# Prefix logsumexp over time: three time steps per partition, exponentials written over the input, chunks interleaved, one DMA queue

## The chip, the cores and the metric

The kernel runs on one core of one Trainium2 chip. The metric is the device time of one execution in microseconds, as the median of several runs. A profile of one execution is shown as well; its span is counted from its first to its last recorded instruction.

## The reference

```python
B, S, D = (4, 4096, 4128)                      # x is float32, normally distributed
out[:, 0, :] = x[:, 0, :].copy()
for t in range(1, S):
    mx = np.maximum(out[:, t - 1, :], x[:, t, :])
    out[:, t, :] = mx + np.log(np.exp(out[:, t - 1, :] - mx) + np.exp(x[:, t, :] - mx))
```

For every batch and column the output at time t is the logarithm of the sum of exp(x) over all times up to t. The kernel computes it as Ln(prefix sum of Exp(x)). Input and output are 270.53 MB each, so at least 541 MB cross between HBM and SBUF.

## The kernel before

**Tiles.** One tile holds 256 consecutive time steps of one batch, all 4128 columns: partition p holds the two rows 2p and 2p+1 (`R = 2`), which are one contiguous run of 33 KB in HBM. There are 4 batches of 16 tiles, 64 in all. A tile is loaded in float32 into `xt` (pool `xpool`, 5 buffers), its exponentials are written in float16 to `et` (pool `epool`, 2 buffers), and the result is written in float32 back into `xt`, from where it is stored.

**Prefix sum on TensorE.** The columns are cut in four chunks of 1024 (`CH`) and a tail of 32; a matmul covers 512 columns (`MM`), so that every matmul of a chunk comes as a pair. For a chunk, `head` adds into one PSUM tile `pt` (pool `pmain`, 3 buffers[...]): a triangular matrix `incl` times the exponentials of row 0, a strictly triangular `excl` times those of row 1, and, except in the first tile of a batch, `last` times the carry. The carry is a float16 copy of the running sum; `last` picks its partition 127. ScalarE then takes Ln of `pt` into row 0 of `xt` (line 98). `second` adds the exponentials of row 1 with an identity (`ident`), takes Ln into row 1 (line 105), and VectorE copies `pt` to the carry (line 106). The 32-column tail does the same in a small PSUM tile `qt` (lines 124 and 125). All matmuls are recorded under the helper `mm`, line 80.

**Order of the work.** `tc.manual_schedule()` keeps each engine's instructions in the order in which the program emits them. The main loop emits for each tile: its load on SP's DMA queue (line 135), one Exp over the whole tile of 2 x 4128 columns on ScalarE (line 139), and then the scan of the tile before. Within a scan, `head` of chunk c is emitted ahead of `second` of chunk c-1. The store is issued on the queue of GpSimd (POOL) at the end of the scan (line 126). A load waits until the store that used its buffer five tiles before has landed.

Of the kernel before, what the change touches and what calls it, by code (L numbers as in the profile page):

```python
# [1 line left out]

# [4 lines left out]

FP32 = mybir.dt.float32
FP16 = mybir.dt.float16
ACT = mybir.ActivationFunctionType  # L10
P = 128
R = 2
CH = 1024
MM = 512


def _constants(nc, pool):


    def tri(base, name):  # L20
        t = pool.tile([P, P], FP16, name=name)
        nc.gpsimd.memset(t, 1.0)

        nc.gpsimd.affine_select(  # L24
            out=t, in_=t, pattern=[[1, P]], compare_op=mybir.AluOpType.is_ge,
            fill=0.0, base=base, channel_multiplier=-1,
        )
        return t

    def ones_where_zero(base, mult, step, name):  # L30
        t = pool.tile([P, P], FP16, name=name)
        nc.gpsimd.memset(t, 0.0)
        nc.gpsimd.affine_select(  # L33
            out=t, in_=t, pattern=[[step, P]], compare_op=mybir.AluOpType.not_equal,
            fill=1.0, base=base, channel_multiplier=mult,
        )
        return t

    return (
        tri(0, "incl"),  # L40
        tri(-1, "excl"),
        ones_where_zero(0, 1, -1, "ident"),
        ones_where_zero(-(P - 1), 1, 0, "last"),
    )


@with_exitstack
def kernel(
    ctx: ExitStack,
    tc: tile.TileContext,  # L50
    x: bass.AP,
    out: bass.AP,
):

    nc = tc.nc
    B, S, D = x.shape
    rows = P * R
    n_t = S // rows  # L60
    assert S % rows == 0
    n_main = D // CH
    tail = D - n_main * CH
    t0 = n_main * CH

    nc.scalar.preload_act_table_set("natural_log_exp_and_others")  # L66
    consts = ctx.enter_context(tc.tile_pool(name="consts", bufs=1))
    incl, excl, ident, last = _constants(nc, consts)

    xpool = ctx.enter_context(tc.tile_pool(name="xpool", bufs=5))  # L70
    epool = ctx.enter_context(tc.tile_pool(name="epool", bufs=2))
    cpool = ctx.enter_context(tc.tile_pool(name="cpool", bufs=1))
    pmain = ctx.enter_context(tc.tile_pool(name="pmain", bufs=3, space=bass.MemoryType.PSUM))
    ptail = ctx.enter_context(tc.tile_pool(name="ptail", bufs=2, space=bass.MemoryType.PSUM))

    carry = [cpool.tile([P, CH], FP16, name=f"carry{c}") for c in range(n_main)]
    carry_t = cpool.tile([P, tail], FP16, name="carry_t") if tail else None

    def mm(pt, w, rhs, start, stop):
        nc.tensor.matmul(pt, lhsT=w, rhs=rhs, start=start, stop=stop, skip_group_check=True)  # L80

    def scan(b, k, xt, et):
        first = k == 0

        def head(c):
            pt = pmain.tile([P, CH], FP32, name="pt")
            for s in range(0, CH, MM):
                o = pt[:, s:s + MM]
                seg = slice(c * CH + s, c * CH + s + MM)
                mm(o, incl, et[:, 0, seg], True, False)  # L90
            for s in range(0, CH, MM):
                o = pt[:, s:s + MM]
                seg = slice(c * CH + s, c * CH + s + MM)
                mm(o, excl, et[:, 1, seg], False, first)
            if not first:
                for s in range(0, CH, MM):
                    mm(pt[:, s:s + MM], last, carry[c][:, s:s + MM], False, True)
            nc.scalar.activation(xt[:, 0, c * CH:(c + 1) * CH], pt, ACT.Ln)  # L98
            return pt

        def second(c, pt):
            for s in range(0, CH, MM):
                seg = slice(c * CH + s, c * CH + s + MM)
                mm(pt[:, s:s + MM], ident, et[:, 1, seg], False, True)
            nc.scalar.activation(xt[:, 1, c * CH:(c + 1) * CH], pt, ACT.Ln)  # L105
            nc.vector.tensor_copy(carry[c], pt)  # L106

        prev = None
        for c in range(n_main):
            pt = head(c)  # L110
            if prev is not None:
                second(c - 1, prev)
            prev = pt
        if tail:
            qt = ptail.tile([P, R, tail], FP32, name="qt")
            seg = slice(t0, D)
            for j in range(R):
                mm(qt[:, j, :], incl, et[:, 0, seg], j == 0, False)
                mm(qt[:, j, :], incl if j else excl, et[:, 1, seg], False, first)
                if not first:  # L120
                    mm(qt[:, j, :], last, carry_t, False, True)
        second(n_main - 1, prev)
        if tail:
            nc.scalar.activation(xt[:, :, t0:D], qt, ACT.Ln)  # L124
            nc.vector.tensor_copy(carry_t, qt[:, 1, :])  # L125
        nc.gpsimd.dma_start(  # L126
            out=out[b, k * rows:(k + 1) * rows, :].rearrange("(p j) d -> p j d", j=R), in_=xt,
        )

    ctx.enter_context(tc.manual_schedule())  # L130
    work = [(b, k) for b in range(B) for k in range(n_t)]
    pending = None
    for b, k in work:
        xt = xpool.tile([P, R, D], FP32, name="xt")
        nc.sync.dma_start(  # L135
            out=xt, in_=x[b, k * rows:(k + 1) * rows, :].rearrange("(p j) d -> p j d", j=R),
        )
        et = epool.tile([P, R, D], FP16, name="et")
        nc.scalar.activation(et, xt, ACT.Exp)  # L139
        if pending is not None:  # L140
            scan(*pending)
        pending = (b, k, xt, et)
    scan(*pending)


# [1 line left out]
_INS = ['x']  # L147
_OUTS = [((4, 4096, 4128), 'float32')]


# [23 lines left out]
```

## Time and profile before

| What | us |
|---|---|
| Median of 9 runs (range) | 1270.41 (1269.3 to 1271.51) |
| The profiled execution | 1270.15 |
| Its span | 1268.4 |
| ScalarE (ACT) busy | 948.7 |
| TensorE (PE) busy | 611.4 |
| VectorE (DVE) busy | 313.8 |
| GpSimd (POOL) busy | 36.0 |

The page of the profile begins with busy time by engine, then cuts the span into 40 slices with the busy tenths of each engine and of the DMA engines and the rate in GB/s, lists the DMA queues, follows the chain of work that ended last, and then gives groups of equal instructions with their count, busy time, mean duration and what ended the idle time before them. A busy engine is not by itself the bound: what counts is whose end the others wait for.

### The profile page before, as it was taken

The page shows a single profiled execution, that of the slowest core. Times are in us where ns is not written, and L with a number is a line of the kernel's source. Part 1 is how long each engine was busy: PE and PEld are TensorE (multiplying, and loading weights), DVE is VectorE, ACT ScalarE, POOL GpSimd, SP SyncE. Part 2 cuts the span into 40 slices and gives each one's busy share as a digit, 9 for nine tenths or more (in the row PEclk, how much of TensorE's full clock was granted, in tenths as well). Part 3 has the DMA queues.
Part 4 walks back from the last instruction along what each step waited for, and adds up shares of the span by engine and source line. Part 5 has one row for each costly group of instructions (what it writes and reads, how often), then busy time and mean ns, then how long its engine had stood idle before and what let it go on. Part 6 is the DMA issues. An engine that isn't in the chain of part 4 may idle for free.

```text
span 1268.4 us, 6438 instructions
## 1 busy us (share of the span) xinstructions
PE 611.4 (48%) x2392; PEld 242.6 (19%) x2392; DVE 313.8 (25%) x320; ACT 948.7 (75%) x641; POOL 36.0 (3%) x76
## 2 busy tenths in 40 slices
PE   1565354464454544644536445455353554544543
PEld 0222121121121211212212122121121221211211
DVE  0332132231222322312223122132231222312213
ACT  5987777777777777777777777767777777677774
POOL 0000000000000000000000000000000000000000
PEclk9787786877867777778778687786877877768777
DMA  9999999999999999999999999999999999999996
GB/s 401 428 417 432 433 432 433 433 433 433 431 433 432 433 433 432 433 433 433 433 433 432 433 432 433 433 433 433 432 432 433 433 432 433 433 432 432 433 411 274
DMA packets 18463, 541.47 MB, mean 427 GB/s; under 512 B 2048, under 2 KB 2048, under 8 KB 2048
## 3 DMA queue, kind: packets, MB, share of 16 engines
q1 hardware_dynamic: 9216, 270.54, 49.6%
q0 software_dynamic: 9216, 270.54, 49.5%
q8 instruction: 18, 0.29, 0.1%
q14 instruction: 13, 0.11, 0.0%
HBM read 270.53 MB, written 270.53 MB: 427 GB/s over the span
## 4 chain that ended last, share of the span: by engine, by line
issue 89%; DMA 6%; POOL 2%; ACT 1%; PE 1%; DVE 0%; POOLq 0%; DVEq 0%; SPq 0%
DMA xt<-in_x_dram 3%; DMA out_dram<-xt 3%; POOL out_dram L126 2%; PE pt L80 1%; ACT xt L98 0%; ACT xt L105 0%; DVE carry L106 0%; POOLq L126 0%; DVEq L169 0%; DVE carry_t L125 0%; ACT et L139 0%; SPq L135 0%; DVEq L125 0%
## 5 line engine op out<-in xcount | busy, mean ns | idle before, releaser
L139 ACT ACTIVATE et<-xt 128x8256 f16<-128x8256 f32 x64 | 453.3, 7083 | 176.8 <-DMA xt<-in_x_dram 176.8
L106 DVE CAST carry<-pt 128x1024 f16<-128x1024 f32 x256 | 307.6, 1222 | 940.4 <-ACT xt L105 940.4
L80 PE MATMUL pt<-et,ident 128*128 128x512 f16 x512 | 197.9, 477 | 599.1 <-ACT xt L98 599.1
L98 ACT ACTIVATE xt<-pt 128x1024 f32<-128x1024 f32 x256 | 254.4, 1019 | 114.9 <-PE pt L80 114.3
L105 ACT ACTIVATE xt<-pt 128x1024 f32<-128x1024 f32 x256 | 255.0, 1026 | 11.6 <-PE pt L80 11.6
L80 PE MATMUL pt<-et,incl 128*128 128x512 f16 x512 | 194.7, 469 | 41.0 <-DVE carry L106 20.5
L80 PE MATMUL pt<-et,excl 128*128 128x512 f16 x512 | 187.6, 454 | 0.0
L80 PEld LDWEIGHTS <-ident 128*128 128x128 f16 x512 | 55.9, 109 | 679.0 <-issue 655.3
L80 PE MATMUL pt<-carry,last 128*128 128x512 f16 x480 | 167.7, 436 | 0.0
L80 PEld LDWEIGHTS <-incl 128*128 128x128 f16 x704 | 74.1, 112 | 152.8 <-issue 116.1
L80 PEld LDWEIGHTS <-excl 128*128 128x128 f16 x576 | 65.0, 113 | 97.8 <-issue 51.7
L80 PEld LDWEIGHTS <-last 128*128 128x128 f16 x600 | 63.8, 108 | 78.8 <-issue 38.6
L126 POOL DMA_DIRECT2D out_dram<-xt x64 | 34.2, 534 | 1216.9 <-ACT xt L124 1216.9
L80 PE MATMUL qt<-et,incl 128*128 128x32 f16 x192 | 17.8, 177 | 0.0
L124 ACT ACTIVATE xt<-qt 128x64 f32<-128x64 f32 x64 | 16.1, 251 | 0.0
L80 PE MATMUL qt<-carry_t,last 128*128 128x32 f16 x120 | 15.1, 176 | 0.0
L125 DVE CAST carry_t<-qt 128x32 f16<-128x32 f32 x64 | 11.6, 181 | 0.0
L80 PE MATMUL qt<-et,excl 128*128 128x32 f16 x64 | 11.3, 176 | 0.0
L66 ACT ACT_TABLE_LOAD x1 | 1.3, 1283 | 0.8 <-PEq L158 0.8
L24 POOL TENSOR_SCALAR_AFFINE_SELECT incl<-incl 128x128 f16<-128x128 f16 x1 | 0.3, 288 | 0.0
L24 POOL TENSOR_SCALAR_AFFINE_SELECT excl<-excl 128x128 f16<-128x128 f16 x1 | 0.3, 287 | 0.0
L33 POOL TENSOR_SCALAR_AFFINE_SELECT ident<-ident 128x128 f16<-128x128 f16 x1 | 0.3, 287 | 0.0
(9 smaller groups left out, 1.5 us busy)
## 6 DMA issues: line engine op xcount, KB each, us to landing
xt<-in_x_dram SPq DMA_DIRECT2D x64, 4128.0 KB, 28.1
out_dram<-xt POOLq DMA_DIRECT2D x64, 4128.0 KB, 33.1
```

The costliest lines, as they stand in the source:

```text
L24: nc.gpsimd.affine_select(out=t, in_=t, pattern=[[1, P]], compare_op=mybir.AluOpType.is_ge, fill=0.0, base=base, channel_multiplier=-1,)
L33: nc.gpsimd.affine_select(out=t, in_=t, pattern=[[step, P]], compare_op=mybir.AluOpType.not_equal, fill=1.0, base=base, channel_multiplier ...
L66: nc.scalar.preload_act_table_set("natural_log_exp_and_others")
L80: nc.tensor.matmul(pt, lhsT=w, rhs=rhs, start=start, stop=stop, skip_group_check=True)
L98: nc.scalar.activation(xt[:, 0, c * CH:(c + 1) * CH], pt, ACT.Ln)
L105: nc.scalar.activation(xt[:, 1, c * CH:(c + 1) * CH], pt, ACT.Ln)
L106: nc.vector.tensor_copy(carry[c], pt)
L124: nc.scalar.activation(xt[:, :, t0:D], qt, ACT.Ln)
L125: nc.vector.tensor_copy(carry_t, qt[:, 1, :])
L126: nc.gpsimd.dma_start(out=out[b, k * rows:(k + 1) * rows, :].rearrange("(p j) d -> p j d", j=R), in_=xt,)
L139: nc.scalar.activation(et, xt, ACT.Exp)
```

## The change

- A tile holds three rows per partition (`R = 3`, 384 time steps, 49.5 KB runs). As 32 groups of 128 rows are not divisible by 3, each batch has ten tiles of three rows and one of two. In the first batch the two-row tile comes first, in the others last. There are 44 tiles.
- `et` is gone. Exp writes float16 into the first half of the bytes that its float32 input chunk occupies in `xt` (a float16 view `half` of the same tile). `xpool` has 4 buffers.
- Exp is issued per chunk (1024 columns, the last one 1056 with the tail), three rows at once: 176 Exp instructions for 64.
- The work is one software pipeline over all chunks of all tiles. Round g emits the Ln of row 2 of chunk g-2, the Ln of row 1 of chunk g-1, the Ln of row 0 of chunk g, each with the identity matmuls for its next row, then Exp of chunk g+2, and then the head matmuls of chunk g+1.
- The carry is kept in two float16 parts, a rounded value in partitions 96 to 127 and the rest in partitions 32 to 63, by a copy and a subtraction of 32 partitions each (`keep`). The matrix `pick` adds partitions 127 and 63. Carries are zeroed at the start.
- The tail's matmuls use broadcast right-hand sides: six for a three-row tile.
- Loads and stores alternate on SP's one DMA queue. Three loads are issued first; then each store is followed by the load of the tile three further on, which goes to the buffer of the tile before the stored one.

```diff
+    bufs = 4
+    xpool = ctx.enter_context(tc.tile_pool(name="xpool", bufs=bufs))
     cpool = ctx.enter_context(tc.tile_pool(name="cpool", bufs=1))
     pmain = ctx.enter_context(tc.tile_pool(name="pmain", bufs=3, space=bass.MemoryType.PSUM))
     ptail = ctx.enter_context(tc.tile_pool(name="ptail", bufs=2, space=bass.MemoryType.PSUM))
     carry = [cpool.tile([P, CH], FP16, name=f"carry{c}") for c in range(n_main)]
...
+    carry_t = cpool.tile([P, tail], FP16, name="carry_t")
+    for t in (*carry, carry_t):
+        nc.vector.memset(t, 0.0)
+    ctx.enter_context(tc.manual_schedule())
+    def mm(pt, w, rhs, start=False, stop=False):
         nc.tensor.matmul(pt, lhsT=w, rhs=rhs, start=start, stop=stop, skip_group_check=True)
...
+    def keep(cr, pt):
+        nc.vector.tensor_copy(cr[HI:HI + 32, :], pt[HI:HI + 32])
+        nc.vector.tensor_tensor(
+            out=cr[LO:LO + 32, :], in0=pt[HI:HI + 32], in1=cr[HI:HI + 32, :],
+            op=mybir.AluOpType.subtract,
+        )
+    class Step:
+        def __init__(self, b, row, r):
+            self.b, self.row, self.r = b, row, r
+            self.first = row == 0
+        def dram(self, t):
+            rows = t[self.b, self.row:self.row + P * self.r, :]
+            return rows.rearrange("(p j) d -> p j d", j=self.r)
+        def load(self):
+            full = xpool.tile([P, R, D], FP32, name="xt")
+            self.xt = full[:, :self.r, :]
+            self.half = self.xt.bitcast(FP16)
+            nc.sync.dma_start(out=self.xt, in_=self.dram(x))
+        def store(self):
+            nc.sync.dma_start(out=self.dram(out), in_=self.xt)
+    class Chunk:
+        def __init__(self, step, c):
+            self.t, self.c = step, c
+            self.w = D - last * CH if c == last else CH
+        def e(self, j, a, b):
+            return self.t.half[:, j, 2 * self.c * CH + a:2 * self.c * CH + b]
+        def exp(self):
+            c0, w = self.c * CH, self.w
+            nc.scalar.activation(
+                self.t.half[:, :, 2 * c0:2 * c0 + w], self.t.xt[:, :, c0:c0 + w], ACT.Exp,
+            )
+        def head(self):
+            t = self.t
+            pt = self.pt = pmain.tile([P, CH], FP32, name="pt")
+            for j in range(t.r):
                 for s in range(0, CH, MM):
...
+                    mm(pt[:, s:s + MM], excl if j else incl, self.e(j, s, s + MM), start=j == 0)
+            if not t.first:
+                for s in range(0, CH, MM):
+                    mm(pt[:, s:s + MM], pick, carry[self.c][:, s:s + MM])
+            if self.c == last:
+                self.tail_head()
+        def tail_head(self):
+            t, r = self.t, self.t.r
+            full = ptail.tile([P, R, tail], FP32, name="qt")
+            qt = self.qt = full[:, :r, :]
+            to = lambda v, n: v.unsqueeze(1).to_broadcast([P, n, tail])
+            for i in range(r):
+                e = self.e(i, CH, CH + tail)
+                mm(qt[:, i:, :], incl, to(e, r - i), start=i == 0)
+                if i:
+                    mm(qt[:, :i, :], excl, to(e, i))
+            if not t.first:
+                mm(qt, pick, to(carry_t, r))
+        def stage(self, j):
+            t, c, pt = self.t, self.c, self.pt
+            nc.scalar.activation(t.xt[:, j, c * CH:(c + 1) * CH], pt, ACT.Ln)
+            if j + 1 < t.r:
+                for s in range(0, CH, MM):
+                    mm(pt[:, s:s + MM], ident, self.e(j + 1, s, s + MM), stop=j + 2 == t.r)
+                if c == last and j == 0:
+                    nc.scalar.activation(t.xt[:, :, t0:D], self.qt, ACT.Ln)
+                    keep(carry_t, self.qt[:, t.r - 1, :])
+            else:
+                keep(carry[c], pt)
+    steps = []
+    for b in range(B):
+        n = S // P
+        parts = [R] * (n // R) + ([n % R] if n % R else [])
+        if b == 0:
+            parts.reverse()
+        row = 0
+        for r in parts:
+            steps.append(Step(b, row, r))
+            row += P * r
+        assert row == S
+    chunks = [Chunk(s, c) for s in steps for c in range(n_main)]
+    ahead = bufs - 1
+    for s in steps[:ahead]:
+        s.load()
+    stored = 0
+    chunks[0].exp()
+    chunks[1].exp()
+    chunks[0].head()
+    for g in range(len(chunks) + R - 1):
+        for d in range(R - 1, -1, -1):
+            if 0 <= g - d < len(chunks) and d < chunks[g - d].t.r:
+                k = chunks[g - d]
+                k.stage(d)
+                if k.c == last and d + 1 == k.t.r:
+                    k.t.store()
+                    if stored + ahead < len(steps):
+                        steps[stored + ahead].load()
+                    stored += 1
+        if g + 2 < len(chunks):
+            chunks[g + 2].exp()
+        if g + 1 < len(chunks):
+            chunks[g + 1].head()
```

In the constants, `R = 3`, `HI, LO = 96, 32`, and `pick` has ones in rows 127 and 63 where `last` had them in row 127. The removed lines, left out here, are those of the kernel printed above.

## Prediction

> **What bounds the kernel now.** I read the 40 slices and the queue table of the page first. In the slices each digit is a busy share in tenths, and the last row is the rate at which the DMA engines moved bytes.
>
> ```profile
> ACT  5987777777777777777777777767777777677774
> DMA  9999999999999999999999999999999999999996
> GB/s 401 428 417 432 433 432 433 433 433 433 431 433 432 433 433 432 433 433 433 433 433 432 433 432 433 433 433 433 432 432 433 433 432 433 433 432 432 433 411 274
> DMA packets 18463, 541.47 MB, mean 427 GB/s; under 512 B 2048, under 2 KB 2048, under 8 KB 2048
> q1 hardware_dynamic: 9216, 270.54, 49.6%
> q0 software_dynamic: 9216, 270.54, 49.5%
> ```
>
> The DMA engines are full from end to end. Loads (q1) and stores (q0) take half each, and the rate is 432 to 433 GB/s. ScalarE, the busiest engine, is at seven tenths. Next, the waits:
>
> ```profile
> ACT et L139 <- DMA xt<-in_x_dram: 176.8, 61, 11.2
> SPq L135 <- DMA out_dram<-xt: 1174.5, 59, 60.2
> ```
>
> ScalarE waits for a load before almost every Exp; SP holds each load until an earlier store has landed. So compute waits for data and data for the DMA engines. The floor is bytes over rate: 2 x 270.53 MB / 433 GB/s = 1249.6 us. The span is 1268.4, so 18.8 us lie above it. The stretches of the end (engines' busy time and count, TensorE clock, DMA share, GB/s) show where:
>
> ```profile
> 1230.00:1235.00 5.00, 0.01 (x1) 0.01 (x1) 0.00 (x0) 5.00 (x3) 0.00 (x0) 0.64 1.06 456
> 1235.00:1240.00 5.00, 5.00 (x16) 1.91 (x16) 1.23 (x1) 3.37 (x4) 0.00 (x0) 0.67 0.23 99
> 1240.00:1245.00 5.00, 4.07 (x24) 1.87 (x23) 3.68 (x4) 4.34 (x6) 0.53 (x1) 1.00 0.25 107
> 1245.00:1250.00 5.00, 3.87 (x19) 1.66 (x17) 2.34 (x2) 3.95 (x5) 0.00 (x0) 1.00 1.00 429
> ...
> 1255.00:1260.00 5.00, 0.00 (x0) 0.00 (x0) 0.00 (x0) 0.00 (x0) 0.00 (x0) 0.53 0.99 423
> ```
>
> From 1235 to 1245 the engines ran at a quarter: 10 x (1 - 0.24) = 7.6 us lost. The timeline says why (start, duration, engine, line):
>
> ```profile
> 1226.94 7.08 ACT L139 ACTIVATE et<-xt 128x8256 f16<-128x8256 f32 x1 [2.09 <-DMA xt<-in_x_dram]
> 1233.93 1.92 ACT L98 ACTIVATE xt<-pt 128x1024 f32<-128x1024 f32 x2
> ...
> 1243.61 0.53 POOL L126 DMA_DIRECT2D out_dram<-xt  x1 [17.93 <-ACT xt L124]
> ```
>
> The last load has landed at 1226.9, its whole-tile Exp is done before the scan of tile 63 begins, and the store of tile 63 goes out only at 1243.61, after all earlier transfers are through. The other parts: the first load's Exp starts at 13.3, against 9.76 us for its 4.23 MB at 433 GB/s, so 3.5 us of start; the last packets end near 1264.1 by the one-microsecond stretches, so 4.3 us of landing and closing; 18.8 - 7.6 - 3.5 - 4.3 leaves 3.4 us of small shortfalls (slices 2 and 3, and a share of 0.95 to 0.98 from 1206 to 1230).
>
> **What the Trainium skill says.** "DMA: Bandwidth & Descriptors", section Where 436 GB/s comes from, gives a ceiling of 435.2 GB/s for the sixteen engines; the trace agrees, with 433 in a stretch of 1100 us (100 to 1200). The same page, Issuing engines are not separate DMA queues, says that transfers issued from several engines share those sixteen; the trace agrees, with q1 and q0 at 49.6 and 49.5%. Its section Queues, rings and completion order says that an engine goes round-robin between queues packet by packet; so read and write packets already alternate on each engine at 433 GB/s, though the trace doesn't show the order. Its section Anatomy of one DMA calls the bubble of the completion write tiny (about one cycle); the trace shows the first loads, five on one queue, landing at 13.3 and 23.06 (starts of their Exps), 9.76 us apart, which is exactly 4.23 MB at 433.
>
> **The change, part by part.**
>
> *Bytes.* Unchanged: 1249.6 us at 433. A three-row tile is 128 x 3 x 4128 x 4 B = 6.34 MB, 14.64 us each way, 29.28 us for load and store; a two-row tile 9.76 and 19.5. The runs grow from 33 to 49.5 KB. What that is worth isn't in the trace: at most the 435.2 ceiling, 1243.2 us, a gain of 6.4; a loss I bound at 431 GB/s (the lowest full slice from the fourth to the 38th), +5.8. I take none.
>
> *One queue for both directions.* It removes GpSimd's 64 issues (34.2 us busy, none waited for by ScalarE). On SP each store waits for the last Ln of its tile, and behind it stands the load of the tile three on; who waits for that load is ScalarE, three tiles later. The engines never run dry if store s is issued before load s+2 has finished. By queue order load s+2 ends 29.28 us after load s+1. Last Ln of tile s: its rounds are held by the Exps of the first two chunks of tile s+1, so it ends some 2.8 + 2 x 5.9 + 1 = 15.6 us after load s+1 has landed (prices below). Cover: 13.7 us per tile. The buffer of load s+3 was freed by store s-1, ahead in the same queue. The cost of passing from store to load on one queue isn't shown: loads back to back and the last two stores back to back (429 and 423 GB/s above) show no gap. I take 0 for 88 transfers; the bound above is 0.25 us each (a fifth of a 33 KB packet's 1.22 us), 22 us; a gain beyond the ceiling is excluded.
>
> *ScalarE.* From these rows (busy, mean ns):
>
> ```profile
> L139 ACT ACTIVATE et<-xt 128x8256 f16<-128x8256 f32 x64 | 453.3, 7083 | 176.8 <-DMA xt<-in_x_dram 176.8
> L106 DVE CAST carry<-pt 128x1024 f16<-128x1024 f32 x256 | 307.6, 1222 | 940.4 <-ACT xt L105 940.4
> L105 ACT ACTIVATE xt<-pt 128x1024 f32<-128x1024 f32 x256 | 255.0, 1026 | 11.6 <-PE pt L80 11.6
> ```
>
> 7083 and 1026 ns for 8256 and 1024 columns give 0.84 ns a column and 0.17 us fixed. Exp of 3 x 1024 columns: 2.75 us; 2.8 with the tail. Per chunk of three rows: 2.75 + 3 x 1.03 = 5.9 us; per tile 4 x 5.9 + 0.3 for the tail's Ln = 23.8. The budget is 29.28. The 112 extra Exps cost 112 x 0.17 = 19 us of ScalarE, all beside transfers: 40 x 23.8 + 4 x 16.2 = 1017 us of work under 1249.6. Nothing on the path.
>
> *TensorE and VectorE in a round.* Matmuls per row stay the same: 12 per three-row chunk for 8 per two-row one. Pairs take 0.85 us in the timeline where the clock is low (1217.03 to 1217.89), 0.43 where it is high. The tightest loop is Ln of row 0, identity pair, eight head matmuls, next Ln of row 0: 1.03 + 0.04 + 0.85 + 3.4 + 0.2 = 5.5 us at the low clock. The head needs the PSUM buffer that `keep` frees. Its copy is at most L106's 1.22 us; the subtraction has no row: between 0.6 and 2.4 us (half and twice L106), I take 1.2. With 2.4 the buffer comes 1 us later than the identity pair ends, 6.5 us a round. The six tail matmuls add under 1 us once in four rounds. All under 7.32 us, a quarter of 29.28. If that cover is gone, every microsecond over it counts 176 times.
>
> *Start.* The first tile has two rows as before and lands at the same time: 3.5 us stay. Three loads (16.9 MB) keep the engines busy until about 42; store 0 goes out near 37: load 1 lands at 13.3 + 14.64 = 27.9, then an Exp, two Lns and an Exp, and the last Ln, 2.8 + 2.1 + 2.8 + 1. No hole.
>
> *End.* Queue order is load 43, stores 41, 42, 43. Let T be the landing of load 43. Store 41 is issued at T-24.4 + 15.6 = T-8.8 and runs from T to T+14.6. Tile 42 is finished near T+12, store 42 runs to T+29.3. Tile 43, two rows, needs 4 short Exps (1.9 us) interleaved with Lns and then three rounds bound by the loop: T+26. Store 43 follows without a gap. So the 7.6 us hole goes; what is late next is the landing and the close, 4.3, as before. Cover is 2 to 3 us; if it is missed, up to 3 us come back.
>
> *Sum, on the profiled execution:* 3.5 + 1249.6 + 4.3 = 1257.4; of the 3.4 us of small shortfalls I keep 1. Span 1258.4; with the 1.75 us that lie around the span (1270.15 - 1268.4), 1260.1. The profiled 1270.15 is 0.26 below the median, so I say 1260.3.
>
> **The rivals.** (1) *The hole only shrinks.* Rounds near the end run at 6.5 us and the small shortfalls stay: +2.4, and 3 us of hole come back: 1266. For it: the cover is thin. Against: the four two-row chunks are short. (2) *Slower: a gap at each change of transfer on one queue.* Before, when one queue waited for the completion of its transfer, the other had packets; now nothing fills it. Place: between a store and the next load in each engine. Price: 88 x 0.25 = 22 us, 1282. It turns the gain of 10 into a loss from 10/88 = 0.11 us each. Against it: loads alone and stores alone ran without a gap. (3) *Slower: the in-place Exp is tied to its neighbours.* If the waits cover the whole span of the three-row view, Exp of chunk g+2 waits for the identity pair and the head for that Exp: 5.5 + 2.75 + 0.4 = 8.7 us a round at the low clock, 6.5 at the high one; at 8.0, 176 rounds less the four short tiles give about 1370. It decides from 7.3 us. For it: no such view is in the kernel before. Against: the bytes touched are disjoint. (4) *A lower rate:* the hole goes, but the larger pieces run at 431: 1266 with nothing else, 1271, which is no change, together with (1). Half of its chance goes to each. Nothing in the profile speaks for it but that 49.5 KB runs are not in it.
>
> **How the numbers follow.** Forecast 0.70 (1253 to 1263: the ceiling rate with none of the shortfalls, to the rate of before with all of them); (1) 0.10; (4) 0.06; (2) 0.08; (3) 0.06. 0.2% is 2.5 us, about what a measurement here can tell from no change. Faster by more (under 1267.9): 0.70 + 0.10 + 0.03 = 0.83; within: 0.03; slower: 0.14. The range takes the forecast, (1) and (4): 1253 to 1269, which holds 0.83.
>
> **What would show it.** Right: 433 GB/s in all slices up to the last two, no hole before the last stores, all packets on one queue, ScalarE waiting for loads, SP's stores issued over 5 us before the transfer ahead ends. Wrong: the rate dips at each change of transfer (2); ScalarE's Exp waits for TensorE and the DMA share falls to 0.9 (3); a low share in the last 40 us (1).

## The result and the profile after

The kernel after takes 1262.89 us (median of 9 runs, 1262.80 to 1263.22) against 1270.73 for the kernel before (29 runs): a ratio of 0.9939, 95% interval 0.9931 to 0.9947. It is 7.8 us faster; 10.1 were forecast (1260.3 against the 1270.41 of the runs shown then), and the time lies in the range. The profiled execution took 1262.82 us, its span is 1261.1.

The slices, the queues and the transfers of the page after:

```profile
ACT  5997777777777777778569777777966977777784
...
DMA  9999999999999999999999999999999999999998
GB/s 411 410 442 433 429 429 437 434 427 431 440 435 426 432 436 435 431 428 434 437 431 436 434 428 435 437 430 431 433 432 435 435 428 434 431 432 435 434 417 350
...
q1 hardware_dynamic: 12672, 541.07, 99.4%
q8 instruction: 18, 0.29, 0.1%
...
xt<-in_x_dram SPq DMA_DIRECT2D x40, 6192.0 KB, 42.2
out_dram<-xt SPq DMA_DIRECT2D x40, 6192.0 KB, 28.1
```

All data is on one queue now, the rate from 100 to 1200 us is still 433, and the last slice moves 350 GB/s in place of 274. A load takes 42.2 us from issue to landing because two other transfers stand ahead of it: until the end the queue is not short. The waits of ScalarE and of SP's queue (us in total, times, longest):

```profile
ACT xt L128 <- DMA xt<-in_x_dram: 248.0, 42, 12.2
...
ACT xt L167 <- PE pt L88: 45.5, 44, 1.1
...
ACT xt L162 <- PE pt L88: 0.7, 1, 0.7
```

```profile
SPq L116 <- ACT xt L162: 1177.8, 44, 30.0
SPq L113 <- DMA out_dram<-xt: 14.3, 4, 4.9
```

ScalarE still waits mostly for loads; the tail's Ln (L167) waits about 1 us a tile for TensorE, the other Lns almost nothing, and no Exp waits for TensorE. SP waits for a tile's last Ln (44 stores), hardly for a store. The groups that the prediction priced:

```profile
L128 ACT ACTIVATE xt<-xt 128x3072 f16<-128x3072 f32 (+3 forms) x176 | 478.4, 2718 | 248.0 <-DMA xt<-in_x_dram 248.0
L162 ACT ACTIVATE xt<-pt 128x1024 f32<-128x1024 f32 x512 | 487.6, 1030 | 2.5 <-PE pt L88 0.7
L92 DVE CAST carry<-pt 32x1024 f16<-32x1024 f32 x176 | 216.4, 1230 | 761.3 <-ACT xt L162 761.1
L93 DVE TENSOR_TENSOR carry<-pt,carry 32x1024 f16<-32x1024 f32 x176 | 215.9, 1227 | 6.1
```

The end, in stretches (engines' busy time and count, TensorE clock, DMA share, GB/s), and the landing of the last load as ScalarE sees it with the last two stores on SP's queue:

```profile
1225.00:1230.00 5.00, 2.28 (x10) 0.69 (x8) 2.41 (x4) 4.32 (x6) 0.00 (x0) 1.00 0.76 327
1230.00:1235.00 5.00, 3.94 (x10) 1.23 (x10) 2.88 (x4) 5.00 (x6) 0.00 (x0) 0.66 0.50 211
1235.00:1240.00 5.00, 2.68 (x11) 0.99 (x11) 4.89 (x4) 4.29 (x4) 0.00 (x0) 1.00 0.76 327
1240.00:1245.00 5.00, 1.97 (x12) 0.76 (x10) 4.82 (x6) 3.19 (x4) 0.00 (x0) 0.92 1.10 476
```

```profile
1220.84 1.91 ACT L128 ACTIVATE xt<-xt 128x2048 f16<-128x2048 f32 x1 [1.34 <-DMA xt<-in_x_dram]
```

```profile
1233.70 0.34 SPq L116 DMA_DIRECT2D out_dram<-xt  x1
...
1244.20 0.33 SPq L116 DMA_DIRECT2D out_dram<-xt  x1
```

A hole in the mean share is still there, 5 x (0.24 + 0.50 + 0.24) = 4.9 us, although store 42 went out 12.9 us after the last load had landed, close to the 12 that were forecast.

**A view by engine.** The Trainium skill says ("DMA: Bandwidth & Descriptors", section Why a DMA increments its semaphore by 16 and not by 1) that each of the sixteen engines of a transfer adds its own increment when its part has landed. The trace agrees: 1408 landings for 88 transfers. Their times show how far the engines have drifted apart. I worked these from the traces (us; "spread" is from the first to the last of the sixteen landings of a transfer; tiles are counted from 0, so the store at 1243.61 that the prediction calls that of tile 63 is store 62 here):

```
                        widest   three transfers from the end   last     span end
kernel                  spread   first to last landing          landing  less it
before                   13.9    1236.4 to 1242.9               1265.0   3.4
after                     7.6    1228.0 to 1235.7               1260.3   0.8
```

The last column, from the last landing to the end of the span, is called the close below. For the kernel before, the middle column is store 61, for the kernel after store 41: the last one before the stores that follow the last load's tile. In the kernel after the first engine is through with store 41 at 1228.0 and the last at 1235.7, and store 42 was issued at 1233.70. The early engines idle (that is the hole), the late one hardly: 14.84 us lie between the last landings of stores 41 and 42, and a three-row tile takes 14.64. In the kernel before, store 61 was through on the last engine at 1242.9 and store 62 issued at 1243.61; its packets started at 1244.7. From this I put the idle time of the late engine at 1.8 us (1242.9 to 1244.7), which is the figure in the expectations below. The landings give 2.6: 12.35 us lie between the last landings of stores 61 and 62, and 9.72 between those of 62 and 63. Either way it is not 7.6.

The 13.9 us of the kernel before are not its lag, that is, the time by which the last engine is behind the first. They belong to stores that run while loads run beside them, and the landings of those loads lie within 6.6 us. At the end, where load 63 and store 60 were all that was queued, the first engine was through with both at 1223.9 and the last at 1233.0: a lag of 9.1 us, against 7.6 in the kernel after.

### The profile page after: what moved, and what is told of

It is laid out like the page before. It is cut to its first block, busy times and chain, and to the rows that moved or that the text cites. A ratio compares the mean times of both kernels' runs of the same rounds, so it can differ in the third digit from the quotient of the medians.

```text
span 1261.1 us, 6165 instructions
## 1 busy us (share of the span) xinstructions
PE 685.4 (54%) x2268; PEld 235.8 (19%) x2268; DVE 451.4 (36%) x445; ACT 947.3 (75%) x733; POOL 2.2 (0%) x13
## 2 busy tenths in 40 slices
DMA packets 12702, 541.46 MB, mean 429 GB/s; under 512 B 1408, under 2 KB 1408, under 8 KB 1408
## 4 chain that ended last, share of the span: by engine, by line
DMA 69%; ACT 21%; PE 5%; issue 2%; DVE 1%; SPq 0%; ACTq 0%
DMA xt<-in_x_dram 64%; ACT xt L128 11%; ACT xt L162 10%; PE pt L88 5%; DMA out_dram<-xt 5%; DVE carry L92 1%; DVE carry L93 1%; ACT xt L167 0%; SPq L116 0%; ACTq L231 0%; SPq L113 0%; ACTq L128 0%; PE qt L88 0%
## 5 line engine op out<-in xcount | busy, mean ns | idle before, releaser
L128 ACT ACTIVATE xt<-xt 128x3072 f16<-128x3072 f32 (+3 forms) x176 | 478.4, 2718 | 248.0 <-DMA xt<-in_x_dram 248.0
L88 PE MATMUL pt<-xt,ident 128*128 128x512 f16 x672 | 250.9, 470 | 533.7 <-ACT xt L162 533.2
L92 DVE CAST carry<-pt 32x1024 f16<-32x1024 f32 x176 | 216.4, 1230 | 761.3 <-ACT xt L162 761.1
L88 PE MATMUL pt<-xt,excl 128*128 128x512 f16 x672 | 244.5, 500 | 0.0
L93 DVE TENSOR_TENSOR carry<-pt,carry 32x1024 f16<-32x1024 f32 x176 | 215.9, 1227 | 6.1
L88 PE MATMUL pt<-xt,incl 128*128 128x512 f16 x352 | 151.7, 525 | 23.9 <-ACT xt L128 15.1
L88 PEld LDWEIGHTS <-excl 128*128 128x128 f16 x756 | 91.9, 124 | 139.6 <-issue 105.5
L88 PE MATMUL pt<-carry,pick 128*128 128x512 f16 x320 | 109.1, 427 | 0.0
L88 PEld LDWEIGHTS <-incl 128*128 128x128 f16 x480 | 45.0, 111 | 130.4 <-DVE carry L93 95.3
L88 PEld LDWEIGHTS <-pick 128*128 128x128 f16 x360 | 40.6, 113 | 56.4 <-issue 33.0
L167 ACT ACTIVATE xt<-qt 128x96 f32<-128x96 f32 (+1 forms) x44 | 10.9, 249 | 45.5 <-PE pt L88 45.5
## 6 DMA issues: line engine op xcount, KB each, us to landing
xt<-in_x_dram SPq DMA_DIRECT2D x40, 6192.0 KB, 42.2
```

Source lines behind the costliest of these rows:

```text
L92: nc.vector.tensor_copy(cr[HI:HI + 32, :], pt[HI:HI + 32])
L93: nc.vector.tensor_tensor(out=cr[LO:LO + 32, :], in0=pt[HI:HI + 32], in1=cr[HI:HI + 32, :], op=mybir.AluOpType.subtract,)
L128: nc.scalar.activation(self.t.half[:, :, 2 * c0:2 * c0 + w], self.t.xt[:, :, c0:c0 + w], ACT.Exp,)
L167: nc.scalar.activation(t.xt[:, :, t0:D], self.qt, ACT.Ln)
```

## The experiments

Theory 1, formed on these landings: every engine has a fixed sixteenth of each transfer, so the engine that is furthest behind sets the time, and idle time of the others in the mean share costs nothing. Theory 2 is that of the prediction: lost mean share is lost time. A further question is which part of the change gives the gain.

**The end of the kernel after, in pieces.**

```diff
+        def store_cols(self, a, b):
+            nc.sync.dma_start(out=self.dram(out)[:, :, a:b], in_=self.xt[:, :, a:b])
...
-                if k.c == last and d + 1 == k.t.r:
+                if k.t in steps[-2:]:
+                    if d + 1 == k.t.r:
+                        k.t.store_cols(k.c * CH, D if k.c == last else (k.c + 1) * CH)
+                elif k.c == last and d + 1 == k.t.r:
                     k.t.store()
```

> The kernel after, but the last two tiles are stored chunk by chunk (four stores each, as each chunk's last Ln is done), so that the stores of tile 42 start some 9 us earlier. In the profile after, the mean DMA share falls to 0.76, 0.50 and 0.76 from 1225 to 1240, which is 4.9 us of all sixteen engines. Theory 1 (the slowest engine sets the time: its last packet of store 41 ends only at about 1235, just when store 42 comes): no more than 0.5 us gained, 1262.4 to 1263.2; the pieces of 12 KB runs may even cost 1 us. Theory 2 (the mean share counts, as in the prediction): 4 to 5 us gained, about 1258.5.

Measured 1271.36 us, 8.5 slower than after; neither theory. This edit made a wait of its own:

```profile
ACT xt L131 <- DMA out_dram<-xt: 18.2, 1, 18.2
```

The Exp of tile 43's last chunk stood 18.2 us until the store of the same tile's first chunk had landed, though the two touch different columns. As a test of the hole it is void. It was repeated with tile 42 alone in pieces:

```diff
-                if k.t in steps[-2:]:
+                if k.t is steps[-2]:
```

> The kernel after with only tile 42 stored chunk by chunk, tile 43 in one piece, so that no Exp comes after a store of its own tile (in the run with both tiles in pieces an Exp waited 18.2 us for a store). The first piece of store 42 is ready some 9 us before the slowest engine is through with store 41. Theory 1 (slowest engine): nothing to gain, 1262.4 to 1264 (pieces of 12 KB run at 4 KB a packet). Theory 2 (mean share): the 4.9 us of mean share lost from 1225 to 1240 come back, about 1258.5.

Measured 1263.81 us (1263.54 to 1263.93), 0.9 above after and nothing gained: theory 1. The hole was filled all the same:

```profile
1225.00:1230.00 5.00, 3.70 (x10) 1.14 (x9) 1.95 (x5) 3.90 (x5) 0.00 (x0) 0.66 0.96 411
1230.00:1235.00 5.00, 3.93 (x10) 1.17 (x10) 2.92 (x3) 5.00 (x6) 0.00 (x0) 0.71 0.88 359
1235.00:1240.00 5.00, 2.16 (x9) 0.80 (x9) 4.87 (x5) 4.81 (x5) 0.00 (x0) 0.95 1.02 410
```

The mean share of these 15 us is 0.95 in place of 0.67, yet the last landing came at 1261.0 in place of 1260.3. The pieces move in packets of 4 KB, of which an engine's 96 take 15.4 us where 8 of 49.5 KB take 14.6, so they cost 0.8 us themselves and could not have hidden a gain of 4 to 5.

**The end of the kernel before.** First the scan of tile 62 ahead of the Exp of tile 63:

```diff
+        if (b, k) == work[-1]:
+            scan(*pending)
+            nc.scalar.activation(et, xt, ACT.Exp)
...
```

> The kernel before, but for the last tile the scan of tile 62 is emitted ahead of the Exp of tile 63, so that store 62 is issued some 9 us earlier (about 1234 in place of 1243.6) and the hole of 7.6 us mean DMA share at 1235 to 1245 goes. Theory 1 (slowest engine): the last landing of an earlier transfer is at 1242.9, so only 1243.6 + 1.1 - 1242.9 = 1.8 us of idle time were on the slowest engine: 1268.5 to 1269.3. Theory 2 (mean share): 5 to 7.6 us gained, 1263 to 1266.

Measured 1269.84 us, a ratio of 0.9989 (0.9977 to 1.0001): inconclusive. Store 62 went out at 1234.76, but store 63 only at 1253.79, after store 62 had landed on all engines (1252.5), so that an idle stretch came back there (12.7 us between the last landings of stores 62 and 63). Next, the same with the last Exp in four pieces among the last scan:

```diff
...
+    def exp(c):
+        if c < n_main:
+            seg = slice(c * CH, D if c == n_main - 1 else (c + 1) * CH)
+            nc.scalar.activation(et[:, :, seg], xt[:, :, seg], ACT.Exp)
...
+    exp(0)
+    exp(1)
+    scan(b, k, xt, et, after=lambda c: exp(c + 2))
```

> The kernel before with another end alone: for the last tile the scan of tile 62 goes ahead of its Exp, and its Exp is four pieces among the scan of tile 63, so that store 62 is issued 8 us after load 63 has landed and store 63 some 21 us after, both before the engines are through with what is queued. The hole of 7.6 us mean share at 1235 to 1245 goes. Theory 1 (slowest engine): 1.8 us gained, 1268.5 to 1269.3. Theory 2 (mean share): 5 to 7.6 us gained, 1263 to 1266.

Measured 1267.94 us, a ratio of 0.9982 (0.9972 to 0.9991): 2.7 us gained, by the interval 1.1 to 3.6. The mean share shows a hole as large as before, now at the last store:

```profile
1245.00:1250.00 5.00, 2.62 (x16) 1.10 (x15) 2.45 (x2) 3.96 (x6) 0.00 (x0) 1.00 0.14 61
1250.00:1255.00 5.00, 0.00 (x0) 0.00 (x0) 2.45 (x3) 1.07 (x3) 0.53 (x1) 0.64 0.64 271
```

Yet store 63 was issued at 1251.37, before the late engine was through with store 62 (1253.0), and the last landing came at 1262.8 in place of 1265.0. The gain is that of the late engine, which by its landings had lost 2.6 us (1.8 was the expectation of theory 1), not the 5 to 7.6 of theory 2.

**Parts of the change.** Two rows in the kernel after:

```diff
-R = 3
+R = 2
-    bufs = 4
+    bufs = 6
```

> The kernel after with two rows per partition and six buffers (the same bytes in SBUF): 33 KB packets, 64 loads and 64 stores. In the two profiles a 33,024-byte packet takes 1222 ns and a 49,536-byte one 1829 ns: 1024 packets an engine take 1251.4 us, against 1248.8 us for the mix of after. Theory 1 (packet size is part of the gain): 2.5 us slower than after, about 1265.4. Rival 2 of the prediction (each change of transfer on one queue costs something): 40 more transfers at 0.25 us add 10 us, about 1275. If packets and transfers are both indifferent: 1262.9.

Measured 1264.38 us (1263.85 to 1264.74): 1.5 slower than after, between the 2.5 expected for the shorter packets and nothing. Even if all of it fell to the forty more transfers, it would be 1.5 / 40 = 0.04 us each, so the gap that rival 2 put at 0.25 isn't there.

Two queues in the kernel after:

```diff
         def store(self):
-            nc.sync.dma_start(out=self.dram(out), in_=self.xt)
+            nc.gpsimd.dma_start(out=self.dram(out), in_=self.xt)
```

> The kernel after with its stores issued by GpSimd, so that loads and stores are on two queues as before. Theory 1: the span after ends 1.3 us after the last packet, that of before 3.8 us, because the last store was GpSimd's; so this costs 2.5 us: about 1265.4. The rate stays. Rival (the single queue itself gives the gain in the steady part, by its order): it loses most of the 7.8 us: 1268 to 1270. Rival (the queue is indifferent): 1262.9.

Measured 1267.34 us, with a wide scatter (1265.83 to 1273.7; the kernel before, too, took 1269.1 to 1278.43 in runs beside the experiments): 4.5 slower, between the two expectations. Its profile is of a run of 1269.42 us. There the span ends 2.6 us after the last landing, against 0.8 in the kernel after, the last load lands later (1225.8 against 1220.8), and store 42 goes out at 1239.04, just after the last engine was through with store 41 (1238.9), so that this engine loses time as well: 16.5 us lie between its landings of stores 41 and 42, in place of 14.8.

The stores on SP's queue in the kernel before, nothing else:

```diff
-        nc.gpsimd.dma_start(
+        nc.sync.dma_start(
             out=out[b, k * rows:(k + 1) * rows, :]
```

> The kernel before with nothing changed but that its stores are issued on SP's queue behind the loads. The order there is load k, store k-1. Theory 1: the close is 2.5 us shorter, but in one queue load 63 comes after store 61, so that nothing is left to transfer while the last whole-tile Exp (7 us) and two scans (9.5 us each) run: store 62 comes some 17 us after load 63 has landed, of which all is idle on every engine: 1276 to 1282, slower than before. The single queue pays only with the finer Exp. Rival (the one queue is itself the gain): 1263 to 1266.

Measured 2464.85 us: slower as expected, but by 1194 us, not by 6 to 11. The reason given was wrong. SP's waits:

```profile
SPq L126 <- ACT xt L124: 2376.2, 64, 39.3
```

Every load is emitted just ahead of its own Exp, and on one in-order queue it now stands behind a store that waits for ScalarE. No load runs ahead any more, and load, Exp, scan and store follow one another. So the order of emission belongs to the queue. With both (`load()` issues the load of the next tile that has none yet):

```diff
...
+    for _ in range(4):
+        load()
...
         if pending is not None:
             scan(*pending)
+            load()
...
+        nc.sync.dma_start(
             out=out[b, k * rows:(k + 1) * rows, :]
```

> The kernel before (two rows, whole-tile Exp, its carry and its scan unchanged) with one part of the change alone: its stores on SP's queue and its loads emitted four tiles ahead, so that store k and load k+4 alternate on the one queue. Tile 62's store is then ready 16.7 us after load 63 has landed, while stores 60 and 61 still need 19.5. Theory 1: the end has no idle stretch on any engine (1.8 us back), and the close is 2.5 to 3 us shorter: 3.5 + 1251.4 (33 KB packets) + 7.5 (lag of the slowest engine) + 0.9 + 1.75 = 1265, the most of the gain. Rival (the finer Exp or the three rows make the gain): 1269 to 1271.

Measured 1262.55 us (1261.48 to 1263.25), a ratio to before of 0.9932 (0.9915 to 0.9949): as fast as the whole change, with two rows, 33 KB runs, the whole-tile Exp, the old carry and the `et` buffers. Page and ScalarE's waits:

```profile
GB/s 403 424 429 433 429 429 432 433 434 435 433 430 431 434 436 434 428 432 432 436 434 432 428 435 434 434 433 434 428 433 436 435 431 428 434 435 434 434 433 362
...
q1 hardware_dynamic: 18432, 541.07, 99.7%
```

```profile
ACT et L149 <- DMA xt<-in_x_dram: 170.9, 58, 11.1
```

Its load 63 lands at 1219.9, 7.0 us earlier than in the kernel before: loads stand ahead of stores that are not ready, and more stores are left for the end, during which the last tiles are computed. Its widest spread is 6.2.

The finer Exp, undone in the kernel after (the four Exps of a tile emitted together):

```diff
...
-        if g + 2 < len(chunks):
-            chunks[g + 2].exp()
+        if g + 2 < len(chunks) and chunks[g + 2].c == 0:
+            for k in chunks[g + 2:g + 2 + n_main]:
+                k.exp()
```

> The kernel after with one part undone: the four Exps of a tile are emitted together, where the first was, in place of one a round. Theory 1 (ScalarE's order lies under the transfers): 0 to 2 us at the end, where store 42 comes a few us later than the slowest engine is through with store 41: 1262.9 to 1265. Rival (the interleaved Exp makes the gain): 1268 to 1271.

Measured 1282.61 us (1280.78 to 1283.51), 19.7 slower: a miss, and an instructive one. Its page and one stretch of the end:

```profile
GB/s 405 380 372 422 425 431 431 434 433 434 427 437 431 434 432 427 432 433 436 420 431 422 419 442 425 440 425 440 420 414 436 425 428 434 433 434 433 431 397 331
```

```profile
661.63 11.22 ACT L128 ACTIVATE xt<-xt 128x3072 f16<-128x3072 f32 x4 [3.94 <-DMA xt<-in_x_dram]
...
1245.00:1250.00 5.00, 4.29 (x14) 1.29 (x12) 3.75 (x5) 3.90 (x6) 0.00 (x0) 0.77 0.05 20
```

The four Exps hold ScalarE for 11.2 us ahead of the last Lns of the tile before, whose store leaves at 682.08, 20.4 us after the load has landed, in place of 15.8 (1212.08 - 1196.24 in the kernel after). A three-row tile leaves 29.3 us for that, the two-row tile at a batch's end 19.5. The rate falls at the start (slices 2 and 3), at a few places between, one of them around the two-row tile whose Exps start at 603.65, and at the end. By the bytes that the packets had moved, it is 8.5 us behind the kernel after at 110 us and 14.6 at 1220. So nearly half is lost at the start, which this count doesn't explain. In this kernel, with three tiles of lookahead, the finer Exp is needed; the two-row kernel with four tiles of lookahead does without it. Whether the size of the tile or the lookahead decides was not separated.

**Transfers alone, and fetches.** First the transfers of the kernel after without its computation:

```diff
-    chunks[0].exp()
-    chunks[1].exp()
-    chunks[0].head()
-    for g in range(len(chunks) + R - 1):
...
+    for s in steps:
+        s.store()
+        if stored + ahead < len(steps):
+            steps[stored + ahead].load()
+        stored += 1
```

> The transfers of the kernel after alone: the same loads and stores in the same order on SP's queue, with the Exp, the matmuls, the Ln and the carries left out, so that a tile is stored as it was loaded. Theory 1 (the slowest DMA engine sets the time, and it is late because instruction fetches and single slow packets fall on it): with almost nothing to fetch the sixteen landings of a transfer stay within about 2 us to the end, in place of 7.5, and the time is 3.5 + 1248.8 + 1.3 + 1.75 and 1 to 2 us of slow packets: 1256 to 1258. Theory 3 (an engine is slower by itself, or the alternation on one queue costs something, whatever runs beside): the spread and the time stay, 1261 to 1263.

Measured 1258.49 us (1257.98 to 1259.4), at the upper end of the expectation, with a spread of 3.3 to 3.8 from 300 us on. So 4.4 us of the kernel after lie above what its transfers take alone, and its spread is 3.8 us wider. Next, those of the kernel before, each tile stored on GpSimd's queue as it was loaded:

```diff
-        et = epool.tile([P, R, D], FP16, name="et")
-        nc.scalar.activation(et, xt, ACT.Exp)
-        if pending is not None:
-            scan(*pending)
-        pending = (b, k, xt, et)
-    scan(*pending)
+        nc.gpsimd.dma_start(
+            out=out[b, k * rows:(k + 1) * rows, :].rearrange("(p j) d -> p j d", j=R), in_=xt,
+        )
```

> The transfers of the kernel before alone: its loads on SP's queue and its stores on GpSimd's, two rows, with the Exp, the matmuls, the Ln and the carries left out, so that a tile is stored as it was loaded. Theory 1: 3.5 + 1251.4 + about 3.7 (spread, as in the one-queue transfers alone) + 3.8 (close of a store of GpSimd) + 1.75 = 1264, some 5 to 6 us above the 1258.5 of the transfers of after alone. Rival (packets, queue and close are indifferent): 1258.5.

Measured 1258.79 us (1258.53 to 1258.93), where 1264 was expected. The close is there (the last landing is at 1253.7, 3.4 us before the end of the span; in one queue 1255.9 and 0.8), but with nothing running beside them 33 KB packets on two queues move no slower, and the spread stays within 2.3. Size of packets and number of queues are not what the kernel before lost by themselves. Last, more instructions to fetch:

> The kernel after with 36 memsets of one column added on idle GpSimd in each round, 6408 in all: about 0.41 MB more to fetch beside 0.39 MB, and no wait for anybody. Theory 1 (instruction fetches on the DMA engines make one engine late): 15 to 25 us more of fetching spread over sixteen engines, 1 to 1.5 us on the average one and 2 to 4 on the slowest: 1264.5 to 1267, with a spread of the last landings of 9 to 12 us in place of 7.5. Theory 3 (fetches are indifferent): 1262.9.

```diff
+    idle = cpool.tile([P, 1], FP16, name="idle")
...
+        for _ in range(36):
+            nc.gpsimd.memset(idle, 0.0)
         if g + 2 < len(chunks):
             chunks[g + 2].exp()
```

Measured 1291.89 us (1290.59 to 1292.73), 29 us slower in place of 2 to 4: the direction of theory 1, ten times the size. Its queues:

```profile
DMA packets 12752, 541.87 MB, mean 420 GB/s; under 512 B 1408, under 2 KB 1408, under 8 KB 1408
...
q14 instruction: 62, 0.51, 0.1%
q8 instruction: 18, 0.29, 0.1%
```

Fifty more fetches of 8 KB came in than in the kernel after, 0.1% of the engines' time in the mean. By the landings they fell on one engine: at 359 us fifteen engines landed within 6.1 us and the sixteenth 6.0 us after them, a spread of 12.1, and the 18 further fetches that had come by then took 5.6 us. Up to 400 us hardly anything was lost by this: by the bytes moved, the engines in the mean were 0.5 us behind the kernel after. At about 13 us the spread stopped growing, near the cover of 13.7 us that the prediction worked out. From there the mean falls behind, by 2.8 us at 500 us, 9.4 at 600 and 22.9 at 1000, as it should if stores come too late for the early engines and all move at the pace of one. ScalarE and VectorE were busy as long as in the kernel after (947.4 and 451.5 us against 947.3 and 451.4). Two things stay open. That the fetches fell on one engine is read from the landings (the records of packets don't name engines), and fetches weren't separated from the memsets themselves. And 50 fetches of 0.31 us are 16 us even on one engine, so the other 13 of the 29 us are not accounted for.

## Why the prediction was right

It was right in direction, time and range, and its bound held: 433 GB/s from 100 to 1200 us, as before. The price of its main step was wrong, and that the sum is near is in part luck. By its steps:

- *Bytes and rate.* Held. Longer runs were taken at nothing. With two rows on one queue, the kernel before with the new queue order is as fast as the change and the kernel after is 1.5 us slower, so they are worth no more than that here.
- *Start.* Held: store 0 was put near 37 us and went out at 37.20.
- *One queue.* Held: 0 taken, at most 0.04 us a transfer measured. The cover was worked out as 15.6 us after the landing; 15.8 measured. Rival 2 falls.
- *ScalarE.* Held: an Exp of 2.75 us forecast, 2.76 in the timeline; a Ln of 1.03, 1.030. No Exp waited for TensorE: rival 3 falls, though the 18.2 us wait of an Exp for a store of other columns shows that its mechanism exists where a DMA reads the tile.
- *VectorE.* The subtraction was bounded by 0.6 and 2.4 us, 1.2 taken: 1.227.
- *End.* Store 42 was put at 12 us after the last landing, store 43 at 26; they came at 12.9 and 23.4. The cover of 2 to 3 us held for the last engine, which store 42 reached 2.0 us before it was through, and not for the first. Here the term that failed is the price: "So the 7.6 us hole goes". The hole in the mean share was idle time of the early engines. On the engine that ends last it was 2.6 us (2.7 gained when it was taken away from the kernel before), and a hole of 4.9 us is still there and costs nothing (0.9 us lost, none gained, when it was filled).
- *The close.* "4.3, as before" was wrong the other way: the last landing lies 3.4 us before the end with a last store of GpSimd, 0.8 with one of SP. That gave back 2.6 us that the sum didn't have.
- *Small shortfalls.* 1 us was kept of 3.4 without a reason. About the 2.4 us that this took off came, but mostly from a thing that the prediction didn't know, the lag of the slowest engine (below): luck.
- *Signs.* All packets on one queue and ScalarE waiting for loads came as named. "No hole before the last stores" did not, and the sign against it, "a low share in the last 40 us (1)", did: 0.50 to 0.76 from 1225 to 1240. So rival 1 was right that the hole only shrinks and wrong on its price. The time lies 2.6 us above the forecast and 3.1 below that rival's 1266.

The forecast gain was 7.6 us for the hole and 2.4 for the shortfalls. By the landings of the two profiled executions, whose spans are 7.3 us apart, it was 2.4 for the idle time of the late engine (2.6 before, 0.2 after), 2.6 for the close and 2.3 for the rest. So the hole was priced 5.2 us too high and the close 2.6 too low, and the difference is what the sum came out low by. By 1220 us the kernel after was only 0.8 us ahead in bytes moved: the gain is made at the end.

The prediction also gave the gain to the end as a whole and didn't separate the parts. The runs do: the one queue with its loads emitted ahead gives all of it (1262.55). Of its mechanism, end and close account for 2.7 + 2.6 = 5.3 of the 8.1 us (1270.64 - 1262.55). The rest goes with a smaller lag: 9.1 us in the kernel before, 7.6 in the kernel after (1.5 of its 2.3 us of rest; the other 0.8 are the bytes by which it was ahead), 6.1 in the kernel before with the new queue order. The lag doesn't follow the number of queues: it is 8.8 us in the two-row kernel after with one queue, and 7.5 in the kernel after with two. Why an engine falls 6 to 9 us behind beside the computation, and 2.3 to 3.8 where transfers run alone, stays open.

## What to carry to other kernels

Where a kernel is bound by transfers, look at the landings engine by engine before pricing a hole in the mean DMA share: only the engine that is furthest behind counts. On an in-order queue that carries loads and stores, emit the loads some tiles ahead; the same queue without that cost a factor of 1.94. Larger tiles leave fewer tiles of lookahead; with three tiles ahead, the coarse order of the Exps cost 19.7 us here, while two-row tiles with four ahead did without the fine one.

## What was not expected of the hardware

- Instruction fetches have packets among those of the data. 6408 one-column memsets on an idle engine cost 29 us, by the landings through one lagging DMA engine, though their fetches took 0.1% of the engines' time in the mean; 16 us of it are the fetches' own time at most.
- The span ended 3.4 us after the last landing where GpSimd issued the last store (2.6 in one run), and 0.8 where SP did (1.0 and 1.1 in the two runs that stored in pieces).
- VectorE's copy from PSUM took as long on 32 partitions as on 128: 1230 ns for 32 x 1024, 1222 for 128 x 1024.
